# RWKV-7 mixer of an encoder layer: the fp32 products of half of the heads on other quarters of the array

## The chip, the cores and the metric

The kernel runs on one core of one Trainium2 chip, in one launch. The metric is the device time of that launch in microseconds (us); the time given for a kernel is the median of its runs. Engines are named as in the profile: PE is TensorE (its matmuls), PEld its weight loads, DVE is VectorE, ACT is ScalarE, POOL is GpSimd, and SP is the queue that issues most DMAs.

## The reference

One layer on 256 tokens of width 2048: a SwiGLU FFN, two gated token mixers side by side (MLA attention and RWKV-7), cross-attention into 256 memory tokens, and a second FFN, with an RMSNorm before and after each. Only the RWKV-7 branch is touched. Per head (16 heads of width 64) it carries a 64x64 state over the tokens:

```python
def step(state, inp):
    r_t, w_t, k_t, v_t, a_t, b_t = inp
    sa = jnp.einsum('bhvk,bhk->bhv', state, a_t)
    state = (state * w_t[:, :, None, :] + sa[..., None] * b_t[:, :, None, :]
             + v_t[..., None] * k_t[:, :, None, :])
    return state, jnp.einsum('bhvk,bhk->bhv', state, r_t)
```

## The kernel before

Large products are done in split precision: each tile of weights (`wraw`, 128x1024 fp32, loaded by SP) is cast by ACT into a high part `whi` (L317), DVE forms the rest `wlo` (L318), and PE multiplies with both (L409 to L411: three matmuls of 512 columns for each step). `whi` and `wlo` are rings of three tiles, `wraw` has four. A tile serves 12 matmuls.

The recurrence is cut into 8 chunks of 32 tokens (`CHUNK`, `NC`). The 16 heads are 8 pairs: pair p holds heads 2p and 2p+1, on partitions 0 to 63 and 64 to 127. Pairs 0 to 3 are group g=0, pairs 4 to 7 group g=1. All these products are fp32 and small, so PE holds a head's product on a part of its 128x128 array: rows come from the partitions of the operands, columns from the partitions of the result in PSUM. Head h=0 of a pair always has rows and columns 0 to 63 (or a 32-wide part of them), head h=1 rows and columns 64 to 127. For each fp32 matmul the trace has two records.

- `rw_gram` (per group and pair of chunks, 8 rounds): `gr` (L1141) multiplies `bk` by `ar`, `bt` (L1145) transposes `bk` by multiplying with the identity, 16 products each. DVE masks `gr` into G (L1147), ACT copies `bt` back (L1149).
- `rw_inverse`: the 128 triangular 32x32 blocks of G are moved by DMA through memory (`ld`, L1168) so that each lies on one partition (LT), DVE inverts them step by step (L1176, L1179), and the result goes back through `td` (L1180) into G (L1184, 8 DMAs).
- `rw_chain` (per chunk c, 16 products in each step): `po` gets the part from the values (L1212, issued at the end of the chunk before) and from the state S (L1227); ACT copies it into `rhs` (L1231); `pu` (L1237) solves with the inverted block; ACT and DVE copy a half each into `uv` (L1240); `pn` (L1246) is the state's update, which DVE adds and scales (L1253, L1254; L1251 in chunk 0); L1256 completes the output in `po`; ACT copies it to `o` (L1264), and POOL's queue stores it (L1266). POOL's queue also loads the values of a chunk (`rw_values`, L1192).

A program order written by hand sets PE's order here: `weave` alternates the steps of this branch (`hot`) with matmuls of output projection and gate blocks (`fill`). `yield 2.0` means that about 2.0 us of filler follow, at 0.65 us for each step of three matmuls. The orders of DVE and ACT are set by a scheduler from priorities; a block of gate columns is finished there by `gt` (L1344 on DVE, L1345 on ACT) and, for the first four blocks, `ya` (L1400). `after(a, b)` puts instruction a behind b. PSUM tiles of this branch come from two pools with two buffers each, `pss` ("sm": gr, po) and `pst` ("tr": bt, pu, pn).

Of the kernel before, what the change touches and what calls it, by code (L numbers as in the profile page):

```python
# [10 lines left out]
F32 = mybir.dt.float32  # L11
# [54 lines left out]
CST = {"gram": 64, "sel": GP * HEADS_G}  # L66
# [3 lines left out]
def _constants():  # L70
# [3 lines left out]
    out["gram"] = np.where(a[None, :] < 32, b[:, None] < a[None, :] % 32, b[:, None] <= a[None, :] % 32).astype(np.float32)  # L74
# [102 lines left out]
class Layer:  # L177
# [109 lines left out]
    def weights(self, w, nk, c0, n, feed=None, still=False, parts=False):  # L287
# [3 lines left out]
        for k in range(0, nk, kt):  # L291
# [11 lines left out]
            for j, stop in zip(cuts, cuts[1:]):  # L303
# [12 lines left out]
                with self.ahead(self.lead):  # L316
                    cast = nc.scalar.copy(out=hi[:, e], in_=raw[:, e])  # L317
                    self.last_split = nc.vector.tensor_sub(  # L318
                        out=lo[:, e], in0=raw[:, e], in1=hi[:, e].bitcast(F32))
# [700 lines left out]
    def rw_prep(self, pool, g, bon, ready):  # L1020
# [83 lines left out]
        for t in range(NT):  # L1104
            pb = self.pss.tile([P, HEADS_G], F32, tag="sm", name="pb")
            for p in range(GP):
# [3 lines left out]
            nc.vector.tensor_copy(  # L1110
                out=bon[:, t].rearrange("p (h b) -> p h b", h=2)[:, :, GP * g : GP * g + GP],
                in_=pb.rearrange("p (h b) -> p h b", h=2))
# [9 lines left out]
        nc.vector.tensor_mul(bkv[:, :, :, 0, :], v4(ta), v4(e2))  # L1122
        nc.vector.tensor_mul(bkv[:, :, :, 1, :], v4(k), v4(e2))
        nc.vector.tensor_mul(arv[:, :, :, 0, :], v4(kk), e1[:, :, :, 0:CHUNK])
        nc.vector.tensor_mul(arv[:, :, :, 1, :], v4(r), e1[:, :, :, 1:])
# [6 lines left out]
    def rw_gram(self, G, g):  # L1132

        nc = self.nc
        mask = self.c("gram").unsqueeze(1).broadcast_to([P, 2 * GP, 64])
        for cc in range(NC // 2):
            ps = self.pss.tile([P, 2, GP, 64], F32, tag="sm", name="gr")
            pt = self.pst.tile([P, 2, GP, 64], F32, tag="tr", name="bt")
            units = [(e, p, self.half(h)) for e in range(2) for p in range(GP) for h in range(2)]
            for e, p, q in units:  # L1140
                nc.tensor.matmul(  # L1141
                    ps[q, e, p, :], self.bk[q, g, 2 * cc + e, p, :], self.ar[q, g, 2 * cc + e, p, :],
                    start=True, stop=True)
            for e, p, q in units:
                nc.tensor.matmul(  # L1145
                    pt[q, e, p, :], self.bk[q, g, 2 * cc + e, p, :], self.ident[q, q], start=True, stop=True)
            nc.vector.tensor_mul(  # L1147
                G[:, cc, g].rearrange("p e j x -> p (e j) x"), ps.rearrange("p e j x -> p (e j) x"), mask)
            nc.scalar.copy(out=self.bk[:, g, 2 * cc : 2 * cc + 2], in_=pt)  # L1149
            yield 1.3  # L1150

    def rw_inverse(self, pool, G):
# [10 lines left out]
        for g in range(2):  # L1163
            for cc in range(0, 4, 2):
                for q in range(2):
                    rows = slice(64 * q, 64 * q + C)
                    for i in range(cc, cc + 2):
                        nc.sync.dma_start(  # L1168
                            out=ld[q, i, g].rearrange("b s t -> s b t"), in_=gv[rows, i, g, :, :C])
# [11 lines left out]
        for cc in range(4):  # L1181
            for q in range(2):
                rows = slice(64 * q, 64 * q + C)
                nc.sync.dma_start(  # L1184
                    out=gv[rows, cc].rearrange("p g b x -> p (g b) x")[:, :, :C],
                    in_=td[q, cc].rearrange("g b s t -> s (g b) t"))

    def rw_values(self, pool, c):

        uv = pool.tile([P, PAIRS, 64], F32, tag="uv", name="uv", bufs=3)  # L1190
        for h in range(2):
            load = self.nc.gpsimd.dma_start(  # L1192
                out=uv[64 * h + 32 : 64 * h + 64].rearrange("s p v -> s (p v)"),
                in_=self.vsh[c * CHUNK : (c + 1) * CHUNK, h * 512 : (h + 1) * 512])
            if c < 3:
                self.after(load, self.small)
        return uv

    def rw_chain(self, pool, G):
        nc = self.nc  # L1200
        heads = [(p, h) for p in range(PAIRS) for h in range(2)]
        block = lambda rows, c, p, cols: G[rows, c // 2, p // GP, c % 2, p % GP, cols]
        at = lambda h, x: slice(64 * h + 32 * x, 64 * h + 32 * x + 32)
        flat = lambda x: x.rearrange("q p v -> q (p v)")
        S2 = pool.tile([P, 2, PAIRS, 64], F32, tag="e1", name="S")
        S = None
        self.last_o = []

        def from_values(c, uv):
            po = self.pss.tile([P, PAIRS, 64], F32, tag="sm", name="po")  # L1210
            for p, h in heads:
                nc.tensor.matmul(  # L1212
                    po[self.half(h), p, :], block(at(h, 1), c, p, slice(0, 64)), uv[at(h, 1), p, :],
                    start=(p == 0), stop=(c == 0 and p == PAIRS - 1))
# [5 lines left out]
        for c in range(NC):  # L1220
# [3 lines left out]
            if S is not None:  # L1224
                for p, h in heads:
                    rows = self.half(h)
                    nc.tensor.matmul(  # L1227
                        po[rows, p, :], self.ar[rows, p // GP, c, p % GP, :], S[rows, p, :], start=False,
                        stop=(p == PAIRS - 1))
# [4 lines left out]
            pu = [self.pst.tile([P, PAIRS, 64], F32, tag="tr", name="pu") for h in range(2)]  # L1234
            for p, h in heads:
                rows = at(h, 0)
                nc.tensor.matmul(  # L1237
                    pu[h][rows, p, :], block(rows, c, p, slice(0, 32)), rhs[rows, p, :], start=True, stop=True)
            for h, copy in enumerate((nc.scalar.copy, nc.vector.tensor_copy)):
                copy(out=flat(uv[at(h, 0)]), in_=flat(pu[h][at(h, 0)]))  # L1240
# [428 lines left out]
```

## Time and profile before

| | |
|---|---|
| time, median of 3 runs (lowest to highest) | 2236.84 us (2235.6 to 2237.34) |
| time of the profiled execution | 2237.75 us |
| its span, first to last instruction | 2236.0 us |
| outside the span | 1.75 us |
| mean granted TensorE clock | 0.997 |
| gram rounds, first to last | 990.7 to 1018.2 us |
| inversion on DVE, first to last | 1025.9 to 1066.2 us |
| chain, first `pu` to last L1256 | 1081.1 to 1184.6 us |

A row of the timeline gives the start, the length, the engine, the line, the operation with out<-in, its shape, and how many instructions are merged ("x32"); in brackets stands how long the engine sat idle before it, and what released it. A length runs from the first start to the last end. Matmuls overlap: the next one starts long before the last has ended, so the distance of two starts says what a matmul costs PE. A row of a group of instructions ends with their sum of busy time and the mean length of one in ns.

### The profile page before, as it was taken

How to read it: one execution, taken by the hardware profiler on the slowest of the kernel's cores; microseconds unless marked ns; L12 is line 12 of the kernel's file. 1: busy time of each engine (PE TensorE's matmuls, PEld its weight loads, DVE VectorE, ACT ScalarE, POOL GpSimd, SP SyncE). 2: the span in 40 equal slices, each digit the busy share in tenths (PEclk: the TensorE clock that was granted, in tenths of full speed). 3: DMA queues.
4: the chain of work that ended last, by engine and by line, in shares of the span. 5: the costliest groups of instructions: out<-in, count | busy, mean ns of one | idle time of the engine just before them, and what ended most of it. 6: DMA issues, size and time to landing. Idle time of an engine off the chain costs nothing.

```text
span 2236.0 us, 34978 instructions
## 1 busy us (share of the span) xinstructions
PE 2206.6 (99%) x13664; PEld 1968.1 (88%) x13664; DVE 1463.7 (65%) x2137; ACT 1133.9 (51%) x1670; POOL 76.3 (3%) x127
## 2 busy tenths in 40 slices
PE   9999999999999999999999999999999999999997
PEld 8999999988888888888788889988999999998886
DVE  7666666654457677868567766657767667664454
ACT  7555555544446566644334465546555555554443
POOL 0000000000000101000122000000000000000000
PEclk9999999999999999999999999999999999999999
DMA  7666666666666654555647776545666666666664
GB/s 259 221 211 201 202 200 201 202 211 208 207 212 211 219 188 156 166 160 173 221 163 255 252 235 199 170 163 185 199 200 204 199 201 203 200 209 207 209 204 150
DMA packets 137671, 449.27 MB, mean 201 GB/s; under 512 B 24097, under 2 KB 25505, under 8 KB 137249
## 3 DMA queue, kind: packets, MB, share of 16 engines
q1 hardware_dynamic: 131696, 431.94, 59.5%
q0 software_dynamic: 4944, 14.69, 2.0%
q8 instruction: 107, 1.75, 0.3%
q10 hardware_dynamic: 864, 0.40, 0.1%
q14 instruction: 60, 0.48, 0.1%
HBM read 436.48 MB, written 10.49 MB: 200 GB/s over the span
## 4 chain that ended last, share of the span: by engine, by line
PE 88%; DVE 5%; issue 4%; DMA 1%; ACT 1%; POOL 0%; DVEq 0%; ACTq 0%; SPq 0%; POOLq 0%
PE mm L373 31%; PE mm L377 15%; PE mm L409 12%; PE mm L411 12%; PE mm L410 12%; DVE wlo L318 2%; ACT whi L317 1%; DVE X L619 0%; DMA vp<-vraw 0%; DVE tm L1176 0%; PE gr L1141 0%; PE po L1256 0%; DVE TT L1179 0%; PE tr L513 0%; PE pn L1246 0%
## 5 line engine op out<-in xcount | busy, mean ns | idle before, releaser
L318 DVE TENSOR_TENSOR wlo<-wraw,whi 128x1024 fp32r<-128x1024 f32 (+3 forms) x792 | 953.9, 1207 | 620.7 <-ACT whi L317 609.1
L317 ACT CAST whi<-wraw 128x1024 fp32r<-128x1024 f32 (+3 forms) x792 | 817.8, 1034 | 797.4 <-PE mm L411 428.3
L373 PE MATMUL mm<-hT,whi 128*128 128x512 f32 x3280 | 1078.6, 383 | 0.5 <-ACT whi L317 0.5
L377 PE MATMUL mm<-hT,wlo 128*128 128x256 f32 x3280 | 882.2, 274 | 1.1 <-DVE wlo L318 1.1
L373 PEld LDWEIGHTS mm<-hT,whi 128*128 128x128 f32 x3280 | 614.7, 190 | 81.4 <-ACT whi L317 0.8
L377 PEld LDWEIGHTS mm<-hT,wlo 128*128 128x128 f32 x3280 | 630.7, 192 | 8.0 <-DVE wlo L318 2.2
L409 PE MATMUL mm<-whi,mh 128*128 128x512 f32 x680 | 257.7, 379 | 0.0
L410 PE MATMUL mm<-wlo,mh 128*128 128x512 f32 x680 | 257.7, 379 | 0.0
L411 PE MATMUL mm<-whi,ml 128*128 128x512 f32 x680 | 257.7, 379 | 0.0
L410 PE MATMUL mm<-wlo,hT 128*128 128x512 f32 (+2 forms) x512 | 180.7, 353 | 4.8 <-DVE wlo L318 4.6
L409 PE MATMUL mm<-whi,hT 128*128 128x512 f32 (+2 forms) x512 | 183.3, 358 | 1.8 <-ACT whi L317 1.6
L411 PE MATMUL mm<-whi,hT 128*128 128x512 f32 (+2 forms) x512 | 179.1, 350 | 0.3 <-DVE hT L504 0.3
L409 PEld LDWEIGHTS mm<-whi,mh 128*128 128x128 f32 x680 | 128.5, 189 | 18.2
L410 PEld LDWEIGHTS mm<-wlo,mh 128*128 128x128 f32 x680 | 128.5, 189 | 18.2
L411 PEld LDWEIGHTS mm<-whi,ml 128*128 128x128 f32 x680 | 128.5, 189 | 18.2
L385 ACT COPY half<-mm 128x256 f32<-128x256 f32 x206 | 75.6, 368 | 120.4 <-PE mm L373 120.4
L410 PEld LDWEIGHTS mm<-wlo,hT 128*128 128x128 f32 x512 | 97.4, 190 | 18.5 <-DVE wlo L318 9.8
L386 DVE TENSOR_TENSOR half<-half,mm 128x256 f32<-128x256 f32 x206 | 86.1, 419 | 40.9 <-ACT half L385 40.9
L409 PEld LDWEIGHTS mm<-whi,hT 128*128 128x128 f32 x512 | 97.4, 190 | 13.4 <-ACT whi L317 1.8
L411 PEld LDWEIGHTS mm<-whi,hT 128*128 128x128 f32 x512 | 97.6, 191 | 9.9 <-DVE hT L504 0.9
L468 POOL TENSOR_TENSOR rstd<-rstd,mhalf 128x1 f32<-128x1 f32 x22 | 14.4, 664 | 1698.1 <-DVE rstd L466 1698.1
L409 PE MATMUL mm<-whi,mT 128*128 128x512 f32 x128 | 48.7, 380 | 0.0
(304 smaller groups left out, 1779.7 us busy)
## 6 DMA issues: line engine op xcount, KB each, us to landing
wraw<-in_w_ffn_up SPq DMA_DIRECT2D x171, 512.0 KB, 4.0
wraw<-in_w_ffn_gate SPq DMA_DIRECT2D x170, 512.0 KB, 3.6
wraw<-in_w_ffn_down SPq DMA_DIRECT2D x168, 512.0 KB, 4.3
wraw<-in_w_in SPq DMA_DIRECT2D x124, 512.0 KB, 3.8
wraw<-in_w_o SPq DMA_DIRECT2D x32, 512.0 KB, 4.2
wraw<-in_w_ckv SPq DMA_DIRECT2D x32, 512.0 KB, 3.5
wraw<-in_w_oa SPq DMA_DIRECT2D x16, 512.0 KB, 3.6
wraw<-in_w_ob SPq DMA_DIRECT2D x16, 512.0 KB, 4.6
```

Source lines behind the costliest of these rows:

```text
L317: cast = nc.scalar.copy(out=hi[:, e], in_=raw[:, e])
L318: self.last_split = nc.vector.tensor_sub(out=lo[:, e], in0=raw[:, e], in1=hi[:, e].bitcast(F32))
L373: both = lambda: nc.tensor.matmul(ps[j], hi[:, s], self.woven(x[:, k]), start=(k == 0), stop=(k == nk - 1))
L377: nc.tensor.matmul(ps[j][:, 0, :], lo[:, s], self.woven(x[:, k, 0]), start=False, stop=False)
L385: nc.scalar.copy(out=tokens, in_=low)
L386: nc.vector.tensor_add(tokens, tokens, high)
L409: nc.tensor.matmul(ps[t], part(xh, t, k), hi, start=(k == first), stop=False)
L410: nc.tensor.matmul(ps[t], part(xh, t, k), lo, start=False, stop=False)
L411: self.last_mm = nc.tensor.matmul(ps[t], part(xl, t, k), hi, start=False, stop=(k == last))
L468: nc.gpsimd.tensor_tensor(out=r, in0=r, in1=self.mhalf, op=ALU.pow)
```

## The change

1. Quarters. Heads of group 1 write their 64-wide products to the other column half: rows of half h, result in half 1-h (`h ^ g`). So (row half, column half) is (0,0) and (1,1) for group 0 and (0,1) and (1,0) for group 1. Loops run over `(j, g, h)`, so that four products in a row belong to four quarters, where the pairs of a group followed each other before. The outputs of the two groups go to two PSUM tiles.
2. Row groups. Of each head's 64 rows in `uv`, G and `po`, 32 belong to the solved vectors (x=0) and 32 to values and outputs (x=1). `role` swaps the two for group 1, so that four products of 32 rows in a row use four different groups of 32 rows.
3. `rw_gram` does both groups in one round: 32 + 32 products, 4 rounds instead of 8, `yield 2.6` instead of 1.3.
4. Evacuations: `rhs` is copied by ACT (group 0) and DVE (group 1), 128x256 each; `uv` by two 32x256 copies on each engine instead of one of 32x512; `o` by two 128x256 copies on ACT; the additions into S in two halves.
5. L1212 moves behind the copies of `o`, since `po` now takes both buffers of its pool: `yield 1.4` stands ahead of it instead of behind.
6. DMAs: 16 instead of 8 from `td` to G, four instead of two for a chunk's values and for a chunk's output, each half as large.
7. In chunk 0 the `uv` copies are put behind the last cast (ACT) and the last `wlo` (DVE) that the program has issued by then.
8. The mask has two column orders, head order in the weights is changed on the host, and `bon` is written by two copies.

```diff
-                    cast = nc.scalar.copy(out=hi[:, e], in_=raw[:, e])
+                    cast = self.last_cast = nc.scalar.copy(out=hi[:, e], in_=raw[:, e])
...
+    def role(self, i, x, g):
+        o = 64 * i + 32 * (x ^ g)
+        return slice(o, o + 32)
...
-    def rw_gram(self, G, g):
+    def rw_gram(self, G):
...
+        units = [(e, p, g, h) for e in range(2) for p in range(GP) for g in range(2) for h in range(2)]
...
-                    ps[q, e, p, :], self.bk[q, g, 2 * cc + e, p, :], self.ar[q, g, 2 * cc + e, p, :],
+                    ps[g][self.half(h ^ g), e, p, :], self.bk[q, g, 2 * cc + e, p, :],
+                    self.ar[q, g, 2 * cc + e, p, :], start=True, stop=True)
...
-            yield 1.3
+            yield 2.6
...
-                nc.sync.dma_start(
-                    out=gv[rows, cc].rearrange("p g b x -> p (g b) x")[:, :, :C],
-                    in_=td[q, cc].rearrange("g b s t -> s (g b) t"))
+                for g in range(2):
+                    nc.sync.dma_start(
+                        out=gv[self.role(q, 0, g), cc, g, :, self.role(0, 0, g)],
+                        in_=td[q, cc, g].rearrange("b s t -> s b t"))
...
-        heads = [(p, h) for p in range(PAIRS) for h in range(2)]
+        units = [(j, g, h) for j in range(GP) for g in range(2) for h in range(2)]
...
-            nc.scalar.copy(out=rhs, in_=po)
+            for g, copy in enumerate(copies):
+                copy(out=rhs[:, ones(g)], in_=po[g])
...
-            for h, copy in enumerate((nc.scalar.copy, nc.vector.tensor_copy)):
-                copy(out=flat(uv[at(h, 0)]), in_=flat(pu[h][at(h, 0)]))
+            for g, copy in enumerate(copies):
+                for i in range(2):
+                    rows = role(i, 0, g)
+                    solved = copy(out=uv[rows, ones(g)], in_=pu[rows, ones(g)])
+                    if c == 0:
+                        self.after(solved, (self.last_cast, self.last_split)[g])
...
-                for p, h in heads:
-                    rows = self.half(h)
+                for j, g, h in units:
+                    rows = half(h ^ g)
                     nc.tensor.matmul(
-                        pn[rows, p, :], self.bk[rows, p // GP, c, p % GP, :], uv[rows, p, :], start=True, stop=True)
+                        pn[g][half(h), j, :], self.bk[rows, g, c, j, :], uv[rows, GP * g + j, :],
+                        start=True, stop=True)
...
             if c < NC - 1:
                 S = Sn
+                yield 1.4
                 po = from_values(c + 1, uvs[c + 1])
...
-            if c < NC - 1:
-                yield 1.4
```

The first place is PE's order in the first gram round, before; `mm` are filler matmuls, and 64x64 is the size of a product.

```order
L410 MATMUL mm<-wlo,hT 128x512
L411 MATMUL mm<-whi,hT 128x512
L1141 MATMUL gr<-ar,bk 64x64 x16
L1145 MATMUL bt<-ident,bk 64x64 x16
L409 MATMUL mm<-whi,hT 128x512
L410 MATMUL mm<-wlo,hT 128x512
```

The same place of the changed program (its lines are one higher in the filler):

```order
L411 MATMUL mm<-wlo,hT 128x512
L412 MATMUL mm<-whi,hT 128x512
L1149 MATMUL gr<-ar,bk 64x64 x32
L1154 MATMUL bt<-ident,bk 64x64 x32
L410 MATMUL mm<-whi,hT 128x512
L411 MATMUL mm<-wlo,hT 128x512
```

Each round has twice the products, and there are half as many rounds; 12 filler matmuls lie between two rounds instead of 6.

The second place is PE's order around the end of chunk 0, before:

```order
L411 MATMUL mm<-whi,hT 128x512
L1246 MATMUL pn<-uv,bk 64x64 x16
L1256 MATMUL po<-uv,G 32x64 x16
L1212 MATMUL po<-uv,G 64x64 x16
L409 MATMUL mm<-whi,hT 128x512
L410 MATMUL mm<-wlo,hT 128x512
```

In the changed program `pn` is L1269, and L1283 is the former L1256:

```order
L412 MATMUL mm<-whi,hT 128x512
L1269 MATMUL pn<-uv,bk 64x64 x16
L1283 MATMUL po<-uv,G 32x64 x16
L410 MATMUL mm<-whi,hT 128x512
L411 MATMUL mm<-wlo,hT 128x512
```

Nine filler matmuls later, the changed program has the former L1212 and L1227 together, as L1229 and L1244:

```order
L411 MATMUL mm<-wlo,hT 128x512
L412 MATMUL mm<-whi,hT 128x512
L1229 MATMUL po<-uv,G 64x64 x16
L1244 MATMUL po<-S,ar 64x64 x16
L410 MATMUL mm<-whi,hT 128x512
```

The number of places where a group of small products interrupts the filler is three for a chunk, as before.

The third place is DVE's order around the same chunk 0, before; `S<-pn,wc` is the first state.

```order
L318 TENSOR_TENSOR wlo<-wraw,whi 128x1024 x4
L1240 COPY uv<-pu 32x512
L318 TENSOR_TENSOR wlo<-wraw,whi 128x1024 x2
L1344 SCALAR_TENSOR_TENSOR gt<-mm,rstd,g 128x512
L318 TENSOR_TENSOR wlo<-wraw,whi 128x1024 x2
L1251 TENSOR_TENSOR S<-pn,wc 128x512
```

The changed program there:

```order
L319 TENSOR_TENSOR wlo<-wraw,whi 128x1024 x5
L1261 COPY uv<-pu 32x256 x2
L1373 SCALAR_TENSOR_TENSOR gt<-mm,rstd,g 128x512 x2
L1429 SCALAR_TENSOR_TENSOR ya<-gt,ya 128x512
L1276 TENSOR_TENSOR S<-pn,wc 128x256 x2
L319 TENSOR_TENSOR wlo<-wraw,whi 128x1024
```

One more tile of `wlo` stands ahead of the copies of u, and the tile after it stands behind both `gt`, a `ya` and the state, where three tiles stood ahead of the state before. ACT's casts have moved in the same way: five instead of four ahead of the copies of u, and the next one behind them and a `gt`.

More of the change, by code (lines that the diff above doesn't have):

```diff
@@ L1130, in half @@
         return slice(64 * i, 64 * i + 64)
-    def rw_gram(self, G, g):
+    def role(self, i, x, g):
+        o = 64 * i + 32 * (x ^ g)
+        return slice(o, o + 32)
+    def rw_gram(self, G):
         nc = self.nc
-        mask = self.c("gram").unsqueeze(1).broadcast_to([P, 2 * GP, 64])
+        masks = self.c("gram").rearrange("p (g x) -> p g x", g=2)
+        tiles = lambda pool, tag, name: [
+            pool.tile([P, 2, GP, 64], F32, tag=tag, name=name) for g in range(2)]
+        units = [(e, p, g, h) for e in range(2) for p in range(GP) for g in range(2) for h in range(2)]
@@ new lines, in rw_gram @@
+                    self.ar[q, g, 2 * cc + e, p, :], start=True, stop=True)
+            for e, p, g, h in units:
+                q = self.half(h)
+                nc.tensor.matmul(
+                    pt[g][self.half(h ^ g), e, p, :], self.bk[q, g, 2 * cc + e, p, :], self.ident[q, q],
+                    start=True, stop=True)
+            for g in range(2):
+                nc.vector.tensor_mul(
+                    G[:, cc, g].rearrange("p e j x -> p (e j) x"), ps[g].rearrange("p e j x -> p (e j) x"),
+                    masks[:, g : g + 1].broadcast_to([P, 2 * GP, 64]))
+                nc.scalar.copy(out=self.bk[:, g, 2 * cc : 2 * cc + 2], in_=pt[g])
@@ L1200, in rw_chain @@
         nc = self.nc
[L1201 to L1204 removed]
+        units = [(j, g, h) for j in range(GP) for g in range(2) for h in range(2)]
+        block = lambda rows, c, j, g, cols: G[rows, c // 2, g, c % 2, j, cols]
+        role, half = self.role, self.half
+        ones = lambda g: slice(GP * g, GP * g + GP)
+        both = lambda where, tag, name: [where.tile([P, GP, 64], F32, tag=tag, name=name) for g in range(2)]
         S2 = pool.tile([P, 2, PAIRS, 64], F32, tag="e1", name="S")
@@ L1207, in rw_chain @@
         self.last_o = []
+        copies = (nc.scalar.copy, nc.vector.tensor_copy)
         def from_values(c, uv):
-            po = self.pss.tile([P, PAIRS, 64], F32, tag="sm", name="po")
-            for p, h in heads:
+            po = both(self.pss, "sm", "po")
+            for j, g, h in units:
+                rows = role(h ^ g, 1, g)
                 nc.tensor.matmul(
-                    po[self.half(h), p, :], block(at(h, 1), c, p, slice(0, 64)), uv[at(h, 1), p, :],
-                    start=(p == 0), stop=(c == 0 and p == PAIRS - 1))
+                    po[g][half(h ^ g), j, :], block(rows, c, j, g, slice(0, 64)), uv[rows, GP * g + j, :],
+                    start=(j == 0), stop=(c == 0 and j == GP - 1))
             return po
@@ L1241, in rw_chain @@
+            for g, copy in enumerate(copies):
+                for i in range(2):
+                    rows = role(i, 0, g)
+                    solved = copy(out=uv[rows, ones(g)], in_=pu[rows, ones(g)])
+                    if c == 0:
+                        self.after(solved, (self.last_cast, self.last_split)[g])
             yield 2.2
             if c < NC - 1:
-                pn = self.pst.tile([P, PAIRS, 64], F32, tag="tr", name="pn")
-                for p, h in heads:
-                    rows = self.half(h)
+                pn = both(self.pst, "tr", "pn")
+                for j, g, h in units:
+                    rows = half(h ^ g)
@@ L1414, in rwkv @@
                     tc.cur_priority = base
-                    for g in range(2):
-                        yield from self.rw_gram(G, g)
+                    yield from self.rw_gram(G)
                     self.rw_inverse(pool, G)
```

100 lines of the change are left out of this document (52 added, 48 removed).

## The prediction, made before the changed kernel ran

> **What bounds the kernel now.** I read the page's busy shares and its chain first, then the groups of instructions by shape, then the timeline of the RWKV stage.
>
> ```profile
> PE 2206.6 (99%) x13664; PEld 1968.1 (88%) x13664; DVE 1463.7 (65%) x2137; ACT 1133.9 (51%) x1670; POOL 76.3 (3%) x127
> ...
> PE 88%; DVE 5%; issue 4%; DMA 1%; ACT 1%; POOL 0%; DVEq 0%; ACTq 0%; SPq 0%; POOLq 0%
> ```
>
> PE is the bound: busy for 99% of the span and 88% of the chain that ended last. What leaves PE's queue shortens the run, unless PE then waits. The small products come next, by shape:
>
> ```profile
> L1141 PE MATMUL gr<-ar,bk 64*64 64x64 f32 x256 | 9.2, 221 | 0.0
> L1212 PE MATMUL po<-uv,G 32*64 32x64 f32 x256 | 9.2, 220 | 0.0
> L1256 PE MATMUL po<-uv,G 32*32 32x64 f32 x256 | 8.9, 216 | 0.6 <-DVE uv L1240 0.6
> L1227 PE MATMUL po<-S,ar 64*64 64x64 f32 x224 | 8.0, 221 | 0.0
> ```
>
> Seven such groups make about 60 us of PE time. Each record lasts about 0.22 us, but they overlap; what they cost is read from starts. The first gram rounds:
>
> ```profile
> 990.38 0.38 PE L411 MATMUL mm<-whi,hT 128*128 128x512 f32 x1
> 990.69 1.01 PEld L1141 LDWEIGHTS gr<-ar,bk 64*64 64x64 f32 x32 [0.33 <-issue]
> 990.69 1.15 PE L1141 MATMUL gr<-ar,bk 64*64 64x64 f32 x32
> ...
> 991.67 1.10 PE L1145 MATMUL bt<-ident,bk 64*64 64x64 f32 x32
> ...
> 992.71 0.48 PE L409 MATMUL mm<-whi,hT 128*128 128x512 f32 x1
> ...
> 993.02 0.38 PE L410 MATMUL mm<-wlo,hT 128*128 128x512 f32 x1
> ...
> 993.89 0.38 PE L411 MATMUL mm<-whi,hT 128*128 128x512 f32 x1
> ```
>
> In 1.15 us lie 32 records of 0.22 us, so the last starts 0.93 us after the first. Two heads alternate between two quarters, so there are 16 pairs of records, one each 0.058 us (0.93/16). If a pair's pace is set by its quarters, four products on four quarters go in the time of two. That is the central assumption; no row of this trace has four in flight, nor two quarters of one row half.
>
> **The gram rounds.** From 990.38 to 993.89 lie six filler matmuls (0.216 us each, 993.89 less 993.02 being four steps) and one round: 3.51 - 1.30 = 2.21 us. Eight rounds cost 17.7 us. Afterwards four rounds have twice the records, at four instead of two per 0.058 us: 2.21 us each, 8.85 us. **Gain 8.85 us**, of which 1.4 us is that four interruptions are gone (2.21 less 32 pairs of 0.058 is 0.35 each). PSUM has no second buffer now: the next round waits for two masks on DVE and two copies on ACT. At the 128x512 cost that S shows below (0.69 us) this is 1.4 us, against 2.6 us of filler, so it is hidden.
>
> **The chunks.** One chunk's three groups:
>
> ```profile
> 1102.31 1.15 PE L1246 MATMUL pn<-uv,bk 64*64 64x64 f32 x32
> 1103.39 1.08 PE L1256 MATMUL po<-uv,G 32*32 32x64 f32 x32
> ...
> 1104.40 1.15 PE L1212 MATMUL po<-uv,G 32*64 32x64 f32 x32
> ...
> 1105.48 0.48 PE L409 MATMUL mm<-whi,hT 128*128 128x512 f32 x1
> ...
> 1105.80 0.38 PE L410 MATMUL mm<-wlo,hT 128*128 128x512 f32 x1
> ```
>
> Eight pairs fewer save 8 x 0.058 = 0.465 us with 1.15 us groups, and 8 x (1.08 - 0.22)/16 = 0.43 us with 1.08 us groups. There are 8 groups of L1212, 7 each of L1246 and L1227 (22 x 0.465 = 10.2 us), 8 each of L1237 and L1256 (16 x 0.43 = 6.9 us). **Gain 17.1 us.** The interruptions stay three for a chunk. What must hide beside the filler: the copies. Their new shapes I bound by these rows:
>
> ```profile
> L385 ACT COPY half<-mm 128x256 f32<-128x256 f32 x206 | 75.6, 368 | 120.4 <-PE mm L373 120.4
> ...
> L386 DVE TENSOR_TENSOR half<-half,mm 128x256 f32<-128x256 f32 x206 | 86.1, 419 | 40.9 <-ACT half L385 40.9
> ```
>
> I take 0.37 us on ACT and 0.42 on DVE. `po` has both buffers of its pool now, so L1229 waits for two copies of `o`: 0.74 us, behind a cast (1.04 us) at worst 1.8 us, under nine filler matmuls and a start, 2.2 us. That cover has 0.4 us left; without it each chunk would lose what is over. POOL issues four DMAs more per chunk, 2.0 us at the 0.50 us of its row below, in some 10 us; values are loaded a chunk ahead.
>
> **Chunk 0.** Here PE waits in the trace of before:
>
> ```profile
> 1081.13 1.08 PE L1237 MATMUL pu<-rhs,G 32*32 32x64 f32 x32
> 1082.24 0.58 ACT L1240 COPY uv<-pu 32x512 f32<-32x512 f32 x1 [7.73 <-PE pu L1237]
> ...
> 1082.73 2.93 ACT L317 CAST whi<-wraw 128x1024 fp32r<-128x1024 f32 x3
> ...
> 1085.08 0.48 PE L410 MATMUL mm<-wlo,hT 128*128 128x512 f32 x1 [0.78 <-DVE wlo L318]
> ...
> 1088.20 0.75 DVE L1344 SCALAR_TENSOR_TENSOR gt<-mm,rstd,g 128x512 f32<-128x512 f32 x1 [2.04 <-PE mm L411]
> 1088.38 0.63 PE L410 MATMUL mm<-wlo,hT 128*128 128x512 f32 x1
> ...
> 1089.34 1.15 PE L1246 MATMUL pn<-uv,bk 64*64 64x64 f32 x32
> ...
> 1090.52 1.23 DVE L318 TENSOR_TENSOR wlo<-wraw,whi 128x1024 fp32r<-128x1024 f32 x1 [0.44 <-ACT whi L317]
> ...
> 1093.64 0.63 ACT L1345 ACTIVATE gt<-gt 128x512 f32<-128x512 f32 x1 [1.51 <-DVE gt L1344]
> ...
> 1094.31 0.69 DVE L1400 SCALAR_TENSOR_TENSOR ya<-gt,ya 128x512 f32<-128x512 f32 x1 [0.70 <-ACT gt L1345]
> ```
>
> ACT stood 7.73 us at the copy of u while casts waited behind it. The second filler matmul came at 1085.08 instead of 1082.46 (1.01 us for `pu`, 0.32 for a start): 2.6 us. Then matmuls took 0.63 us, and `pn` started 1.7 us later than at the usual pace. Together 4.3 us. After the change this tile is split ahead of the copies, so this wait goes. The next late thing is the tile behind it: on DVE it stands behind both `gt`, a `ya` and two halves of S. Counted from the start of `pn`: the first `gt` ends near 0.2 (its matmuls ended three matmuls earlier), the second at 0.9, `ya` at 1.6, S (2 x 0.42, overlapping) at 2.3, `wlo` at 3.5. PE, with `pn` and L1283 at half length, wants it at 1.5. **It waits 2.0 us: net gain 2.3 us.** Two ends: none (4.3 us gained) and the slow matmuls again (0.6). Those are a matter of the clock:
>
> ```profile
> 1082.20:1085.60 3.40, 1.02 (x5) 0.67 (x4) 2.49 (x3) 3.35 (x4) 0.00 (x0) 1.00 0.24 96
> 1085.80:1089.20 3.40, 3.40 (x9) 2.36 (x8) 1.36 (x3) 0.00 (x0) 0.00 (x0) 0.50 0.81 254
> ...
> 979.00:982.40 3.40, 2.25 (x11) 1.68 (x10) 3.40 (x4) 1.04 (x1) 0.00 (x0) 1.00 0.24 58
> ```
>
> The granted clock (sixth value) was 0.50 for 3.4 us after a stretch with PE busy for 1.02 of 3.40 us, and stayed 1.00 after 2.25 of 3.40. A 2.0 us wait lies between (1.4); I leave the 1.7 us out and keep it in the range. The Trainium skill, "TensorE: Matmul & The Clock Gate", section "What's actually happening", has the clock halved after at least one idle window of about 3.4 us; by that this wait would cost no clock at all. The trace differs: two waits of 1.6 and 0.78 us were enough.
>
> SP has 16 DMAs into G where it had 8:
>
> ```profile
> 1070.85 4.95 SPq L1184 DMA_DIRECT2D G<-td  x8
> 1075.90 16.20 SPq L309 DMA_DIRECT2D wraw<-in_w_in  x8
> ...
> DMA to landing us min/median/max: 2.4/2.9/4.4
> ```
>
> `pu` of chunk 0 needs the first four: 1070.85 + 4 x 0.62 + 4.4 = 1077.7, before 1081.13, hidden by 3.4 us. The weight load behind them moves by up to 4.95 us to 1080.85, lands near 1085.2 and could be `wlo` by 1087.5, just ahead of the 1088 at which DVE gets there.
>
> **The last chunk** gives back:
>
> ```profile
> 1172.02 1.01 POOL L1266 DMA_DIRECT2D osc<-o  x2 [1.33 <-ACT o L1264]
> ...
> 1180.26 0.69 DVE L1287 TENSOR_TENSOR ab<-ab,bon 128x512 f32<-128x512 f32 x1 [3.43 <-DMA ab<-vsh]
> ...
> 1183.59 1.08 PE L1256 MATMUL po<-uv,G 32*32 32x64 f32 x30 [0.60 <-DVE uv L1240]
> ```
>
> DVE's copy of u stands behind `ab`, which waits for a DMA that POOL issues behind the stores of chunk 6. PE already waits 0.8 us for it, with the start. From chunk 6's last group on, PE gets four groups shorter (1.8 us); the DMA gets later by two issues less the earlier copies of `o`, about 0.4 us. PE waits some 3.0 us: **2.2 us lost**; bounds none and, with a half clock, 3.9.
>
> **Sum**, against the profiled execution (span 2236.0, 1.75 outside, 2237.75 us, which is 0.9 above the median of the runs): 2237.75 - 8.85 - 17.1 - 2.3 + 2.2 = 2211.7 us. Both half clocks would give 2215.1; no waits at all 2207.5.
>
> **Rivals.** *Two quarters of one row half do not overlap.* Then the 64x64 products keep their pace; only those on 32 rows gain. Gain: 1.4 us of interruptions, 8 x 0.465 + 16 x 0.43 = 10.6 us, 2.75 us in chunk 0, less 1.7 us in the last chunk: 13.05 us, 2224.7 us. For it: no row shows a shared half in parallel. Against: loads and matmuls of one quarter do run side by side (32 loads in 1.01 us inside the 1.15 us of `gr`), so a half is not held by one of them. The same page, "What overlaps and what doesn't", says that a weight load overlaps with matmuls in flight only if its row group differs; by that this rival wins, at 2224.7. The rows of `gr` already disagree within one quarter.
>
> *PE is fed no faster than one product in 0.058 us.* Nothing in the trace goes faster. Then only interruptions and chunk 0 gain: 1.4 + 3.2 - 0.4 = 4.2 us, 2233.5 us. Against it: 32-row groups of 32x32 go at 0.054, so the pace follows the shape.
>
> *Slower: each change between straight and crossed quarters empties the array.* A start after another shape costs 990.69 - 990.38 = 0.31 us instead of 0.216, so 0.094 us. The 480 products of 64x64 make 240 pairs, each such a change: 22.6 us, less 13.05: 9.5 us slower, 2247.3 us. It decides from 13.05/240 = 0.054 us per change. The Trainium skill, "TensorEngine Tiling (Array Packing)", "Key Properties", has the array drain when the tiling mode changes, not when only the tile does; by that this rival is out. No run here shows it.
>
> **How the numbers follow.** Four at once everywhere 0.60; only on 32 rows 0.20; something between (a partial overlap) 0.07; fed too slowly 0.08; slower 0.05. 0.2% is 4.5 us, about what a measurement of this kernel can tell from no change. So faster 0.87, same 0.08, slower 0.05. The likeliest case alone spans 2207 to 2216. The range takes in the second rival and leaves out the last two: 2207 to 2226.
>
> **What would show it.** Four gram rounds of about 2.2 us; groups of 32 records about 0.6 us long instead of 1.15; in chunk 0 a wait of PE for `wlo` near 2 us behind L1283, none behind `pu`; before the last L1283 a wait of about 3 us for `uv`. If `gr` with 64 records takes 2 us, the first rival holds. A wait at each L1229 for ACT's copies would make the prediction wrong by up to 0.5 us a chunk.

## The result and the profile after

| | before | after |
|---|---|---|
| time, median of 4 runs each (lowest to highest) | 2237.09 us (2235.60 to 2237.81) | 2221.18 us (2217.99 to 2223.53) |
| ratio, 95% interval | | 0.9929 (0.9912 to 0.9946) |
| profiled execution / its span | 2237.75 / 2236.0 us | 2221.88 / 2220.1 us |

The forecast was 2211.7 us, in a range of 2207 to 2226. The time lies inside the range, and about 10 us above the forecast. It lies outside the 2207 to 2216 that the prediction gave its likeliest case alone. The page of the profile after, first its busy times, then its chain:

```profile
PE 2181.4 (98%) x13664; PEld 1943.7 (88%) x13664; DVE 1466.8 (66%) x2164; ACT 1133.8 (51%) x1686; POOL 93.1 (4%) x159
...
PE 86%; DVE 6%; DMA 3%; issue 2%; ACT 1%; POOL 1%; SPq 1%; DVEq 0%; ACTq 0%; POOLq 0%
```

PE has lost 25 us of busy time, close to the forecast's 26 us of shorter work; the slower clock that is shown below makes some of the work that is left longer. But the span is only 15.9 us shorter: PE's share of the chain fell by two points, and that of DMA rose from 1% to 3%. Where the 10 us went shows when the starts of the same PE instructions are set side by side (read from the two timelines):

| stretch on PE | before | after | change | forecast |
|---|---|---|---|---|
| start to the first `gr` | 990.69 | 989.05 | -1.64 | 0 |
| first `gr` to `pu` of chunk 0 | 90.44 | 80.52 | -9.92 | -9.3 |
| `pu` of chunk 0 to `pu` of chunk 1 | 17.38 | 16.84 | **-0.54** | -4.6 |
| on to `pu` of chunk 7 | 80.38 | 68.54 | -11.84 | -13.5 |
| on to the 31st filler step behind it | 24.36 | 29.84 | **+5.48** | +1.3 |
| on to the last step of three matmuls | 1019.25 | 1019.21 | -0.04 | 0 |
| from there to the end of the span | 13.48 | 16.10 | **+2.62** | 0 |
| sum | | | -15.88 | -26.1 |

The first row is scatter: in the profiles of the experiments below, whose gram rounds are reached by the same PE program, the first `gr` starts anywhere from 988.2 to 991.7 us. Three stretches miss the forecast by more than a microsecond or two: chunk 0, the last chunk, and the end of the program.

First what came as forecast. PE's groups of small products after, by shape, from the gram rounds to the end of the chain:

```profile
L1283 PE MATMUL po<-uv,G 32*32 32x64 f32 x256 | 5.9, 227 | 4.6 <-DVE uv L1261 4.6
L1229 PE MATMUL po<-uv,G 32*64 32x64 f32 x256 | 5.9, 232 | 0.0
L1244 PE MATMUL po<-S,ar 64*64 64x64 f32 x224 | 4.9, 224 | 0.0
L1149 PE MATMUL gr<-ar,bk 64*64 64x64 f32 x256 | 4.6, 221 | 0.0
```

One record still lasts 0.22 us, but 256 records now occupy 4.6 to 5.9 us instead of 8.9 to 9.2. The timeline of PE, a gram round and chunk 1:

```profile
989.05 1.16 PE L1149 MATMUL gr<-ar,bk 64*64 64x64 f32 x64
990.04 1.11 PE L1154 MATMUL bt<-ident,bk 64*64 64x64 f32 x64
991.08 0.48 PE L410 MATMUL mm<-whi,hT 128*128 128x512 f32 x1
...
1089.78 0.69 PE L1269 MATMUL pn<-uv,bk 64*64 64x64 f32 x32
1090.41 0.65 PE L1283 MATMUL po<-uv,G 32*32 32x64 f32 x32
```

64 records take the time that 32 took, and a group of 32 takes 0.65 to 0.69 us instead of 1.08 to 1.15. The starts of single records in a `pn` group of before and of after (us after 1102 and after 1100) show the pace itself:

```
before  .475 .482           .534 .540           .592 .599           .650 .657
after   .637 .644 .651 .657 .696 .702 .709 .716 .754 .761 .767 .774 .812 .819 .826 .832
```

Every 0.058 us two records started before, and four start now, 7 ns apart. An undisturbed chunk takes 10.75 us instead of 12.97: 2.22 us saved, where the forecast's terms add up to 2.26.

Now chunk 0. PE's timeline after:

```profile
1069.58 0.65 PE L1255 MATMUL pu<-rhs,G 32*32 32x64 f32 x32
...
1073.57 0.65 PE L1283 MATMUL po<-uv,G 32*32 32x64 f32 x32
1077.09 0.79 PE L410 MATMUL mm<-whi,hT 128*128 128x512 f32 x1 [2.87 <-ACT whi L318]
1078.35 0.80 PE L411 MATMUL mm<-wlo,hT 128*128 128x512 f32 x1 [0.46 <-DVE wlo L319]
1078.94 0.63 PE L412 MATMUL mm<-whi,hT 128*128 128x512 f32 x1
...
1086.42 0.65 PE L1255 MATMUL pu<-rhs,G 32*32 32x64 f32 x32
```

PE does wait behind L1283, but not for `wlo` behind a full DVE: it waits 2.87 us for the cast, and then runs matmuls of 0.63 us. Who keeps the cast is told by SP's queue, and then by ACT and DVE:

```profile
1057.00 0.42 SPq L1192 DMA_DIRECT2D td<-TT  x1
1059.08 0.33 SPq L310 DMA_DIRECT2D wraw<-in_w_in  x1
1064.09 7.91 SPq L1196 DMA_DIRECT2D G<-td  x16
1072.10 10.56 SPq L310 DMA_DIRECT2D wraw<-in_w_in  x7
...
1075.99 1.04 ACT L318 CAST whi<-wraw 128x1024 fp32r<-128x1024 f32 x1 [2.17 <-DMA wraw<-in_w_in]
...
1074.46 0.75 DVE L1276 TENSOR_TENSOR S<-pn,wc 128x256 f32<-128x256 f32 x2
1077.07 1.22 DVE L319 TENSOR_TENSOR wlo<-wraw,whi 128x1024 fp32r<-128x1024 f32 x1 [1.86 <-ACT whi L318]
```

Between 1059.4 and 1072.1 SP issues no weights: it waits until `td` has landed, and then issues 16 DMAs into G. The load behind them lands when the cast starts, at 1075.99. DVE was through with the state at 1075.2 and stood idle for 1.86 us. (In DVE's order before, four tiles of `wlo`, not three, stood between the copy of u and the state.)

The last chunk, PE first, then DVE, then POOL's queue:

```profile
1158.33 0.30 PE L1283 MATMUL po<-uv,G 32*32 32x64 f32 x4
1163.20 1.06 PE L1283 MATMUL po<-uv,G 32*32 32x64 f32 x28 [4.58 <-DVE uv L1261]
...
1159.71 0.69 DVE L1316 TENSOR_TENSOR ab<-ab,bon 128x512 f32<-128x512 f32 x1 [6.64 <-DMA ab<-vsh]
1162.29 0.86 DVE L1261 COPY uv<-pu 32x256 f32<-32x256 f32 x2
...
1146.74 1.21 POOL L1433 DMA_DIRECT2D t1d<-gt  x2 [6.87 <-ACT gt L1374]
1147.95 1.99 POOL L1292 DMA_DIRECT2D osc<-o  x4
1152.37 0.54 POOL L1312 DMA_DIRECT2D ab<-vsh  x1 [1.33 <-DMA t1d<-gt]
```

That is the wait that was forecast, at its place and by its cause, but 4.58 us long. The load of `ab` was issued late by a wait of its own: the program gives POOL's DMAs eight semaphores in turn (111 to 118 in the trace), so each waits until the eighth before it has landed, and with four stores of `o` instead of two that eighth is now the store `t1d`.

In both places the clock fell. Stretches of 3.4 us; the sixth value is the granted clock:

```profile
1072.80:1076.20 3.40, 1.42 (x65) 1.04 (x64) 2.37 (x5) 0.84 (x2) 0.56 (x1) 0.97 0.91 297
1076.20:1079.60 3.40, 2.04 (x4) 1.36 (x5) 2.29 (x3) 2.95 (x5) 1.87 (x4) 0.50 0.96 361
1079.60:1083.00 3.40, 3.40 (x38) 2.32 (x37) 2.06 (x2) 1.04 (x1) 3.13 (x7) 0.53 0.90 256
...
1160.20:1163.60 3.40, 0.40 (x16) 0.40 (x20) 3.29 (x6) 0.00 (x0) 0.00 (x0) 0.66 0.17 45
1163.60:1167.00 3.40, 3.40 (x29) 1.68 (x19) 2.79 (x5) 0.65 (x2) 1.99 (x4) 0.50 0.52 181
```

After PE was busy for only 1.42 of 3.40 us the clock was 0.50 to 0.53 for about 6.8 us. Chunk 0 loses 16.84 - 10.75 = 6.1 us in all, of which 3.3 are waits and the rest is clock.

The last 2.62 us lie behind PE's work. The trace's last records are the engines' drains at the end of the program, and POOL's is the last to end. It takes 8.71 us before and 11.32 us after, and both times the end of the span follows 0.79 us later.

### The profile page after: what moved, and what is told of

Read it like the earlier page. It is cut to its first block, busy times and chain, and to the rows that moved or that the text cites. A ratio compares the mean times of both kernels' runs of the same rounds, so it can differ in the third digit from the quotient of the medians.

```text
span 2220.1 us, 35106 instructions
## 1 busy us (share of the span) xinstructions
PE 2181.4 (98%) x13664; PEld 1943.7 (88%) x13664; DVE 1466.8 (66%) x2164; ACT 1133.8 (51%) x1686; POOL 93.1 (4%) x159
## 3 DMA queue, kind: packets, MB, share of 16 engines
q0 software_dynamic: 5968, 14.69, 2.1%
## 4 chain that ended last, share of the span: by engine, by line
PE 86%; DVE 6%; DMA 3%; issue 2%; ACT 1%; POOL 1%; SPq 1%; DVEq 0%; ACTq 0%; POOLq 0%
PE mm L374 31%; PE mm L378 16%; PE mm L410 11%; PE mm L412 11%; PE mm L411 11%; DVE wlo L319 2%; ACT whi L318 1%; DVE X L620 0%; DVE TT L1191 0%; DVE tm L1188 0%; DMA ab<-vsh 0%; PE tr L514 0%; DMA td<-TT 0%; PE xo L1584 0%; SPq L1196 0%
```

## The experiments

The theory: the products themselves do what was forecast, and 10 us were lost at three places outside the array: SP's queue in chunk 0, POOL's queue in the last chunk, POOL's drain at the end. The rivals stand in the expectations. Each diff is against the changed kernel unless another is named.

**Which order of the products counts** (`e3_g_outer`, `e4_h_outer`). In both `rw_gram` and `rw_chain` only the order of the loops is changed:

```diff
-        units = [(j, g, h) for j in range(GP) for g in range(2) for h in range(2)]
+        units = [(j, g, h) for g in range(2) for j in range(GP) for h in range(2)]
```

> The same products on the same quarters, but the loops run over g outermost: all of group 0 (straight quarters), then all of group 1 (crossed), so two quarters are in turn at a time, not four. Theory A (what counts is that four products in a row lie on four quarters): groups of 32 records take 1.15 us again instead of 0.69, those of 64 records 2.1 instead of 1.16; PE's work grows by 8 x 0.93 + 22 x 0.465 + 16 x 0.43 = 24.5 us, of which the shorter waits in chunk 0 and at the end may give back up to 10. So 2235 to 2246 us. Rival B (it is the new tiles or addresses, not the order): groups stay at 0.69 us, time unchanged near 2221.

```diff
-        units = [(j, g, h) for j in range(GP) for g in range(2) for h in range(2)]
+        units = [(j, g, h) for h in range(2) for j in range(GP) for g in range(2)]
```

> Loops run over h outermost: products in a row alternate between straight and crossed quarter of one row half (gr, bt, L1244) or of one column half (pn), never both halves. Theory A (quarters are independent whichever half they share): 32 records take 1.15 us as with two quarters in the old kernel, 64 records 2.1 us, about the time of the kernel with g outermost. Rival B (two quarters of one row half do not overlap, the first rival of the prediction): gr and L1244 take about 2 us for 32 records (0.116 us for a pair of records of each product, 4 us for 64), pn with shared columns 1.15 us; then 64x64 groups of gr, bt and L1244 add another 0.9 us each for 32 records, some 20 us over the kernel with g outermost.

Measured: 2232.56 us with g outermost and 2234.77 us with h outermost (one run each). PE's timeline in chunk 2, first with g outermost:

```profile
1101.10 0.97 PE L1244 MATMUL po<-S,ar 64*64 64x64 f32 x32
1104.80 0.90 PE L1255 MATMUL pu<-rhs,G 32*32 32x64 f32 x32
```

and with h outermost:

```profile
1101.48 0.97 PE L1244 MATMUL po<-S,ar 64*64 64x64 f32 x32
1105.17 0.90 PE L1255 MATMUL pu<-rhs,G 32*32 32x64 f32 x32
```

The groups are equal to 0.01 us, and an undisturbed chunk takes 12.08 us in both. So it makes no difference whether the two quarters in turn lie on a diagonal or share a row half: rival B of the second run, which was the prediction's first rival too, falls. The gain needs four quarters in turn. A miss in size: the groups take 0.97 us and not 1.15. The single records show why: the first products of the second half of the loop start 6 ns behind the last of the first half instead of 0.058 us, on the two quarters that stood free, and in three steps four records start together.

**SP's queue in chunk 0** (`e1_g_pool`, then `e6b_late_g_hold`). First, 12 of the 16 DMAs on another queue:

```diff
-                    nc.sync.dma_start(
+                    (nc.gpsimd if cc else nc.sync).dma_start(
                         out=gv[self.role(q, 0, g), cc, g, :, self.role(0, 0, g)],
```

> Twelve of the 16 DMAs from td to G (those of chunks 2 to 7) go out on POOL's queue instead of SP's; the weight loads behind them on SP can leave about 5.9 us earlier. In the changed kernel PE needs 16.84 us from pu of chunk 0 to pu of chunk 1, against 10.74 us for the next chunk: 6.1 us lost. Theory A (the weight load came late because SP was issuing those DMAs): the wait for ACT's cast (2.87 us) and the half clock behind it go, the distance falls to about 11 to 12 us, total 5 to 6 us faster. Rival B (the forecast's: DVE's order, wlo behind gt, gt, ya and S, would have cost about 2 us anyway): 2 to 2.5 us of wait for wlo remain, total about 3 us faster. The scheduler also puts two more casts and splits ahead of the copies of u here, so under A pn may wait for uv instead.

Measured: 2221.24 us (2220.49 to 2223.53), ratio to before 0.9934 (0.9917 to 0.9950): no gain, so neither expectation of the time held. PE's timeline:

```profile
1074.04 0.71 PE L1269 MATMUL pn<-uv,bk 64*64 64x64 f32 x4 [0.78 <-ACT uv L1261]
1076.02 1.02 PE L1269 MATMUL pn<-uv,bk 64*64 64x64 f32 x28 [1.27 <-DVE uv L1261]
```

The wait for the cast went, and the copies of u took its place: the scheduler had put them behind two more tiles, the first of which was cast at 1071.16 us. From `pu` to `pu` it is 15.11 us. The two waits, 2.05 us within 3 us, were enough for the half clock again. And POOL's last drain grew to 12.30 us.

So both had to be held: the 12 DMAs stay on SP but go behind weight loads (they are issued in program order in chunk 1, each put behind the newest load), and the casts of the second to fourth tile behind `pu` go behind ACT's copies of u.

```diff
-                    cast = self.last_cast = nc.scalar.copy(out=hi[:, e], in_=raw[:, e])
+                    self.newest = load; cast = self.last_cast = nc.scalar.copy(out=hi[:, e], in_=raw[:, e])
...
+        def restore(chunks):
+            for cc, q, g in [(cc, q, g) for cc in chunks for q in range(2) for g in range(2)]:
+                move = nc.sync.dma_start(
+                    out=gv[self.role(q, 0, g), cc, g, :, self.role(0, 0, g)], in_=td[q, cc, g].rearrange("b s t -> s b t"))
+                if cc: self.after(move, self.newest)
+        (restore(range(1)), setattr(self, "restore", restore))
...
-                yield 2.0
+                yield 2.0; c == 1 and self.restore(range(1, 4))
...
-                        self.after(solved, (self.last_cast, self.last_split)[g])
+                        self.after(solved, (self.last_cast, self.last_split)[g]); g or setattr(self, "hold", [None, solved, solved, solved])
```

> SP issues only the four DMAs into G that chunk 0 and 1 need ahead of the next two weight loads, and the other 12 behind these; the casts of the three tiles behind the first one are held behind ACT's copies of u, so that no copy of u stands behind a tile that has not arrived. No DMA is moved to POOL. Theory A (SP's 16 DMAs kept the weight load, and in the run with 12 of them on POOL the copies of u stood behind the late tiles): PE's distance from pu of chunk 0 to pu of chunk 1 falls from 16.84 to 11 to 12.5 us, no half clock, POOL's last drain stays at 11.3 us, 4.5 to 6 us faster than the changed kernel. Rival B (the forecast's wait for wlo on DVE): a wait of about 2 us for wlo stays; 3 us faster. Rival C (the loads are late for another reason, DMA bandwidth or the landing of td): the waits stay, no gain.

Measured: 2218.38 us (2216.78 to 2218.69), ratio 0.9917 (0.9902 to 0.9932). SP and PE:

```profile
1064.92 1.81 SPq L1195 DMA_DIRECT2D G<-td  x4
1067.12 0.83 SPq L310 DMA_DIRECT2D wraw<-in_w_in  x2
1068.01 6.36 SPq L1195 DMA_DIRECT2D G<-td  x12
...
1070.46 0.65 PE L1255 MATMUL pu<-rhs,G 32*32 32x64 f32 x32
1074.45 0.65 PE L1283 MATMUL po<-uv,G 32*32 32x64 f32 x32
1075.04 0.48 PE L410 MATMUL mm<-whi,hT 128*128 128x512 f32 x1
1081.21 0.30 PE L1255 MATMUL pu<-rhs,G 32*32 32x64 f32 x4
```

From `pu` to `pu` it is 10.75 us, the undisturbed pace: all 6.1 us are gone, waits and clock. Rival C falls. Rival B is not tested by this, since DVE's order changed with the loads; two tiles of `wlo` now stand ahead of the state and of both `gt`:

```profile
1073.03 2.36 DVE L319 TENSOR_TENSOR wlo<-wraw,whi 128x1024 fp32r<-128x1024 f32 x2 [0.21 <-ACT whi L318]
1075.42 0.76 DVE L1276 TENSOR_TENSOR S<-pn,wc 128x256 f32<-128x256 f32 x2
1076.09 1.40 DVE L1373 SCALAR_TENSOR_TENSOR gt<-mm,rstd,g 128x512 f32<-128x512 f32 x2
```

The profiled execution is 5.1 us shorter than that of the changed kernel; chunk 1 gave back 0.6 us, and the last chunk, which was left as it was, still costs 29.28 us on the fifth row of the first table. The medians differ by 2.8 us only, and the intervals of the two ratios overlap; why the other runs gained less is open.

**Part 7 alone** (`e5_no_after`).

```diff
-                    if c == 0:
-                        self.after(solved, (self.last_cast, self.last_split)[g])
```

> Only part 7 of the change is taken back: the copies of u of chunk 0 may stand ahead of casts and splits of tiles that are already needed. Theory (part 7 removes the old wait behind pu, worth about 2.6 us): PE waits for whi or wlo behind pu of chunk 0 again, 2 to 3 us, and the later wait for the weight load, which starts from a fixed time on SP, is shorter by as much: total within 2 us of the changed kernel. Rival (part 7 only moved the wait): the wait behind pu does not come back.

Measured: 2220.12 us (one run). The wait behind `pu` did not come back: PE's first wait is for the cast, 2.55 us, behind L1283 as before, and the orders of ACT and DVE are the same as with part 7, instruction by instruction. The theory falls. With the other parts in place the scheduler puts a tile more ahead of the copies by itself, and part 7 does nothing.

**DVE's order in the last chunk** (`e2_ab_late`).

```diff
-            self.after(scaled, self.last_S)
+            self.after(scaled, self.last_uv if t else self.last_S)
```

> The first operation on ab for tokens 128 to 255 is put behind DVE's last copy of u of chunk 7, nothing else. In the changed kernel PE waits 4.58 us before the last L1283 and the clock then falls to 0.50. Theory A (DVE stood at ab, waiting for its DMA, with the copy of u queued behind): the wait goes, the clock stays at 1.00, 6 to 6.5 us faster. Rival B (the wait only moves: the next tile's wlo then stands behind ab on DVE): PE waits 1 to 3 us for wlo instead, 3 to 5 us faster. Rival C (uv itself was late): no change.

Measured: 2218.38 us (2217.39 to 2221.84), ratio 0.9920 (0.9906 to 0.9935). The wait of 4.58 us is gone and the clock of the last chunk stays at 1.00, so A's cause holds and C falls: from `pu` of chunk 7 to the 31st filler step 24.28 us instead of 29.84. Some of it moved, as B says: PE waits 1.39 us for `wlo` at 1175.1 us. The median gained 2.8 us, less than either of the two had expected. In this profile chunk 0 was longer than in the changed kernel (19.39 us against 16.84): `td` took 8.2 us to land, and PE waited 5.31 us for the cast.

**Both repairs** (`e7_fixed`, the edits of `e6b_late_g_hold` and `e2_ab_late`).

> Both repairs: the DMAs into G split as before this run, and the first operation on ab of tokens 128 to 255 behind DVE's last copy of u. If both losses are separate, their gains add: 5 us in chunk 0 and 6 us in the last chunk, 2221.2 - 11 = about 2210 us, near the forecast of 2211.7 plus the 2.6 us by which POOL's last drain is longer. If an earlier PE only waits later for the same DMAs, 2214 to 2218.

Measured: 2214.26 us (2210.53 to 2214.76), ratio 0.9894 (0.9878 to 0.9911): at the edge of the second expectation. Chunk 0 takes 10.75 us, so its whole gain is kept; the last stretch takes 25.61, so 4.2 us of the 5.6 that `e2_ab_late` gained there are left. (The medians do not show this: 2.8 us for each repair alone, 6.9 for both.) What is left is on PE and DVE:

```profile
1163.72 0.48 PE L411 MATMUL mm<-wlo,hT 128*128 128x512 f32 x1 [1.08 <-DVE wlo L319]
1167.97 0.48 PE L411 MATMUL mm<-wlo,hT 128*128 128x512 f32 x1 [1.39 <-DVE wlo L319]
...
1161.24 0.69 DVE L1316 TENSOR_TENSOR ab<-ab,bon 128x512 f32<-128x512 f32 x1 [4.46 <-DMA ab<-vsh]
```

DVE still stands at the second `ab`, now with `wlo` behind it.

**The loads of `ab` earlier** (`e9a_ab_loads_early`, against `e7_fixed`).

```diff
-                                scale[n // 7, h] = self.rw_scale(pool, n // 7, h, bon, self.last_o[n - 1])
+                                scale[n // 7, h] = self.rw_scale(pool, n // 7, h, bon, self.last_o[n - 1 - n // 7])
```

> As e7_fixed, and the loads of lnx and ab for tokens 128 to 255 go out behind the output of chunk 5 instead of chunk 6, ahead of the stores t1d and of chunk 6 on POOL. In e7_fixed PE still waits 1.08 and 1.39 us for wlo behind the last chunk, because DVE stands 4.46 us at the second ab, which waits for its load. Theory A (that load is late because POOL issues it behind t1d, four stores and lnx, and each POOL DMA waits for the eighth before it): both waits go, 2 to 3 us faster than e7_fixed. Rival B (the six operations on ab themselves, 4.1 us on DVE, delay wlo): 1 to 1.5 us of wait stays. Rival C (the second load still stands behind the stores of chunk 6, for its buffer): no gain.

Measured: 2212.25 us (2210.20 to 2212.97), ratio 0.9884 (0.9869 to 0.9899). DVE takes both `ab` without a pause, and the last stretch is 23.54 us, 0.8 us less than in the kernel of before:

```profile
1153.38 0.86 DVE L1261 COPY uv<-pu 32x256 f32<-32x256 f32 x2
1154.27 1.29 DVE L1316 TENSOR_TENSOR ab<-ab,bon 128x512 f32<-128x512 f32 x2
```

A holds, but for one wait of 0.67 us for `wlo` that is left behind the last chunk. The intervals of this ratio and of that of `e7_fixed` overlap, so the gain rests on the profiles. The forecast gave 2207.5 us for a kernel without any of these waits; with the 2.6 us of drain that makes 2210.1, and this kernel is 2 us above it.

**POOL's last drain** (`e8_fewer_pool`, `e9b_values_on_sp`, `e10_o_on_act`). In the first, against `e7_fixed`, values and outputs go out on SP:

```diff
-                load = self.nc.gpsimd.dma_start(
+                load = self.nc.sync.dma_start(
...
-                    last = nc.gpsimd.dma_start(
+                    last = nc.sync.dma_start(
```

> As the run before it, and the 32 loads of values and 32 stores of o go out on SP's queue instead of POOL's, so POOL issues 51 DMAs instead of 115. Theory D (POOL's last drain takes 0.082 us for each DMA that POOL has issued: 8.71 us with 83, 11.32 with 115, 12.30 with 127, which gives 0.0816 and 0.0817): the drain takes 11.32 - 64 x 0.0816 = 6.1 us and the end comes 4 to 5 us earlier (from then on SP's own end may decide), about 2205 to 2206 us if SP's waits for copies and buffers do not hold up weight loads. Rival E (the drain's length comes from the program's size or the run): it stays near 11.3 us and nothing is gained. Rival F: SP waits ahead of weight loads and PE waits for them in the chunks, 1 to 3 us a chunk, slower than the run before it.

In the second, against `e9a_ab_loads_early`, only the values do (the first half of that diff).

> As e9a_ab_loads_early, and the 32 loads of values (not the stores of o) go out on SP's queue, so POOL issues 83 DMAs as in the kernel of before. Theory D (0.0816 us of last drain for each POOL DMA): the drain is 8.71 us again, 2.6 us faster than e9a if SP's waits stay off PE's path. Rival F (SP waits for buffers of u ahead of weight loads, as with stores and loads on SP, where PE waited 4.2 us in chunk 1): PE waits for whi or wlo in chunks 1 to 6, and the gain is lost.

In the third, against `e9a_ab_loads_early`, only the outputs move, and to ACT's queue:

```diff
-                    last = nc.gpsimd.dma_start(
+                    last = nc.scalar.dma_start(
```

> As e9a_ab_loads_early, and the 32 stores of o go out on ACT's queue, behind ACT's own copies of o, so POOL issues 83 DMAs. Theory D: POOL's last drain falls from 11.32 to 8.71 us, 2.6 us faster (2209.6 us) if ACT has room for four issues a chunk. Rival F (in-order queues: the cast and the rhs copy that stand behind the stores on ACT come late): PE waits at pu or for whi in most chunks, 0.5 to 1.5 us each, and the gain is lost.

| kernel | DMAs issued by POOL | POOL's last drain |
|---|---|---|
| `e8_fewer_pool` | 51 | 6.09 us |
| before, `e9b_values_on_sp`, `e10_o_on_act` | 83 | 8.71 us |
| after, and all others | 115 | 11.32 us |
| `e1_g_pool` | 127 | 12.30 us |

Theory D holds at all four counts: 0.082 us for each DMA. Bytes do not decide: the three kernels with 83 DMAs move 14.69 or 13.64 MB on this queue. Each DMA that was added or taken away has 32 packets, so a fixed price for each packet would be 0.0026 us; but by that the 3920 packets of `e8_fewer_pool` would take 10.0 us, and they take 6.09. Whether a move pays depends on the queue that takes them over. `e8_fewer_pool` measured 2216.47 us (2215.57 to 2220.45) and `e9b_values_on_sp` 2216.81 (2212.02 to 2218.82): medians 2.2 and 4.6 us above the kernels without the move. The intervals of the ratios overlap in both pairs, but the profiles show rival F: from `pu` to `pu` chunk 1 takes 18.12 and 18.36 us instead of 10.93 and 11.30. In `e8_fewer_pool` PE waits in chunk 1 because SP's weight loads stand behind stores and values, and so do the splits and the copy of u on DVE:

```profile
1088.81 1.12 PE L1269 MATMUL pn<-uv,bk 64*64 64x64 f32 x28 [4.15 <-DVE uv L1261]
```

`e10_o_on_act` measured 2209.51 us (2208.73 to 2211.11), ratio 0.9883 (0.9866 to 0.9899). In its profile PE's last step starts at 2194.56 us, as in `e9a_ab_loads_early`, and the span is 2.6 us shorter. From the first `gr` to that step it is 1.0 us longer, with waits of 0.66 and 0.69 us at `pu` as rival F has them, so ACT's queue seems to have a price too. By its median it is the fastest version, and its interval lies wholly below that of the changed kernel. Against `e9a_ab_loads_early` the ratios are equal within their intervals; that the 2.6 us are there is shown by the profiles alone.

## Why the prediction was right, and where it was wrong

**Four at once: right.** The central assumption, for which no row of before had an example, holds to a few per cent: four products on four quarters go in the time of two. The rival by which two quarters of one row half do not overlap falls with the equal groups of `e3_g_outer` and `e4_h_outer`, and so does the rule by which it would have won at 2224.7 us (the Trainium skill, "TensorE: Matmul & The Clock Gate", "What overlaps and what doesn't"): here loads and matmuls of one row half run side by side. In `pn` of chunk 1 four records start within 0.020 us and last 0.27; the loads of the next four, 0.13 us long, start 0.05 us behind them. PE is fed faster than a product per 0.058 us. The slower rival, an array that drains at each change between straight and crossed quarters, falls too: in `e4_h_outer` every product changes between them, and its groups are no longer than those of `e3_g_outer`.

**The gram rounds: right.** Four rounds, 1.16 us for 64 records; 9.92 us from the first `gr` to `pu` against 9.3.

**The chunks: right but for 1.7 us.** 2.22 us a chunk instead of 2.26. The waits at L1229 that would have been the wrong side did not come. Chunks 5 and 6 gave back 0.6 and 0.8 us; the second is a transpose that now waits 0.75 us for the state, since PE reaches it sooner. In chunk 5 `pn` stops after four records for DVE's copies of u, and the other 28 start at 1135.20, 0.6 us behind the first.

**Chunk 0: the wait was right, its cause and size wrong.** The step that failed is the one on SP's queue: it moved the weight load by the issue time of the 16 DMAs alone (4.95 us allowed, 2.96 measured) and found it "just ahead" of DVE. It left out two things. `td` itself could land later: 7.09 us from its issue to the first DMA into G instead of 4.47. And PE gained more than the chain that leads to `td`: counted from the first `gr`, `pu` came 9.92 us sooner, `td` (issued at 1066.38 before) only 7.74. So the load landed 6.4 us behind the start of `pu`, where the forecast had 4.1. With the wait for `td` and the 16 issues the load left 13.0 us after the one before it (1059.08), and PE reached the tile first.

DVE's order, on which the 2.0 us rested, came as forecast: the state was done 2.27 us behind the start of `pn` (2.3 forecast), and a `wlo` of 1.22 us right behind it would have ended at 3.5. By these rows PE would have waited some 2 us even for a load in time (an estimate); as it was, the load was later still and decided. In `e6b_late_g_hold` all of the 6.1 us are gone, but there DVE's order is another one too, so how they divide between SP's queue and DVE's order stays open. That the old wait behind `pu` went, for which the forecast counted its net gain, is not the work of part 7: `e5_no_after` has it without.

**The clock: the second half of that error.** The forecast left out the half clock for a wait of 2.0 us, since such a wait lay between the two stretches it had. PE idle for 1.98 of 3.40 us halved the clock, and in `e1_g_pool` 2.05 us did; in `e9b_values_on_sp` a single wait of 1.80 us at 1132.5 was enough. In `e7_fixed` 0.97 us did not:

```profile
1167.00:1170.40 3.40, 2.43 (x11) 2.16 (x12) 3.33 (x5) 0.45 (x1) 0.02 (x1) 1.00 0.91 242
```

So the idle window of about 3.4 us that the Trainium skill asks for ("TensorE: Matmul & The Clock Gate", "What's actually happening") is not needed.

**The last chunk: right in place and cause, too small.** The term that was mis-sized is the load of `ab`, forecast to come later by "two issues less the earlier copies of `o`, about 0.4 us". It came later by 1.33 us more, a wait for the eighth DMA before it, and took 7.32 us to land instead of 6.13; with the clock the stretch lost 5.48 us where the forecast had 1.3.

**The end of the program: not in the forecast.** 32 more DMAs on POOL cost 2.6 us at the drain. The forecast counted them as 2.0 us a chunk beside other work, and there they are hidden; the price comes behind PE's last matmul.

**The range: partly luck.** It reached to 2226 to take in the rival of 2224.7 us, and that rival fell. The likeliest case came true for the products and still missed its own 2207 to 2216, by losses that the range was not made for.

## What to carry to other kernels

Where PE is made faster, list what does not get faster with it, in this case a chain of DMA, DVE and DMA and the queue that it blocks, and compare the two arrival times at the next place where they meet. A wait on a queue is charged to everything behind it, here a weight load that left 13.0 us after the one before: four DMAs that are needed soon and twelve that are not should not stand in one row ahead of a load. Splitting a transfer is not free even when the queue that issues it is idle; on POOL each further DMA cost 0.082 us at the end of this program.

## What the runs showed of the hardware

- Small fp32 products: each quarter takes a record per 0.058 us, whichever quarter runs beside it, and four quarters take four records 7 ns apart: 0.65 to 0.69 us for 32 records instead of 1.08 to 1.15.
- POOL's drain at the end of the program grows by 0.082 us for each DMA that POOL has issued, though those that were varied here lie 1.0 to 1.3 ms ahead of it: 6.09, 8.71, 11.32 and 12.30 us for 51, 83, 115 and 127.
- About 2 us without PE work in 3.4 us (1.80 and 1.98 in one wait, 2.05 in two) halved TensorE's clock for 3.4 to 6.8 us, 0.97 did not; so in chunk 0 waits of 3.3 us cost 6.1.
